# Eight of eleven FFN chunks as seven products in three layers, with the low parts of the two plain weight blocks made by an adding DMA

## The chip, the cores and the metric

The kernel runs on one core of a Trainium2 chip. The metric is device time in microseconds (us) of one execution. TensorE is called PE below, VectorE DVE, ScalarE ACT, GpSimd POOL and SyncE SP; SP issues the loads of the kernel before.

## The reference

A decoder trunk with two layers, one of forgetting attention (FoX) and one of multi-head latent attention (MLA), for 256 tokens of 1024 features in float32. Each layer has two feed-forward networks (FFNs) with 2816 inner columns, so there are four FFNs in all, and they are what the change touches:

```python
def swiglu(x, w_in, w_out):
    h = x @ w_in
    gate, up = h[..., :D_FF], h[..., D_FF:]
    return (jax.nn.silu(gate) * up) @ w_out
...
  x <- LN(alpha*x + 0.5*SwiGLU_1(x))
  x <- LN(alpha*x + Mixer(x))
  x <- LN(alpha*x + 0.5*SwiGLU_2(x))
  x <- LN(alpha*x + sigmoid(x Wg + bg) * (p[i] Wp))
```

## The kernel before

**Split operands.** Every matrix product runs in a reduced float32 format, on operands split into a high part (the value rounded to that format) and a low part (value minus high part). A product is three matmuls: high by high, high by low, low by high. So each block of weights passes two engines before PE can use it: ACT writes the high part (`activation`, Copy, L242 or L250), then DVE subtracts it from the raw block to give the low part (L243 or L254). Both land in one of ten weight slots hl0 to hl9, which PE frees as it goes. Raw groups of 2048 columns (1 MB) arrive by SP's queue into three buffers named raw.

**Chunks.** The 2816 inner columns are cut into 11 chunks of 256. `HT` computes a chunk's gate and up products in turn (gate half, then up half, on PE's `h` and `tr` banks); ACT applies silu to the gate half (L799), DVE multiplies by the up half (L805). The output product of a chunk, its 256 columns by a 256 by 1024 piece of `w_out`, is done in one of two ways:

- plain (`W`): 24 matmuls of 512 columns, at the end of the FFN, on tiles named g and hl;
- summed (`sums`): the 2 by 2 block product as seven products instead of eight, 21 matmuls of 512 columns. For that DVE makes sums and differences of the chunk's blocks (L820, L824, L825, tile P), and ACT and DVE split the result of 896 columns into a *form* (L603 high, L607 low), which stands in one of the home tiles ota, otb, qk and fs. DVE also makes sums of weight blocks by three adds: L274 (1024 columns, into the tile ts), L280 (512, ts) and L282 (512, back into columns 0 to 511 of raw).

The weights of a summed chunk are four units. Unit 0 is columns 0 to 1023 of raw *after* the third add has overwritten their first half; unit 1 is the plain columns 1024 to 2047; units 2 (1024 columns) and 3 (512) are the sums in ts. `WS_ORDER` says in which order PE uses them, and the same order is that in which ACT and DVE prepare them: 1, 0, 2, 3.

**Stages of one FFN.** The chunks come in groups. After the first group PE runs the *first sums*, after the second group (chunks 5, 6, 7) the *second sums*, and then the third group (8, 9, 10), whose chunks are plain. The first FFN of all (*cold*) has chunks 0, 1, 2 plain and sums 3, 4, then 5, 6, 7. The second FFN of layer 0 and that of layer 1 sum 0, 2, 3, 4, then 5, 6, 7, with chunk 1 plain. The first FFN of layer 1 (*kv*) sums 2, 3, 4, then 5, 6, 7, with 0 and 1 plain and three homes. So a sums stage ends with the form of the chunk whose up half PE has finished last, and that chunk's multiplication, form and weights are made while PE runs the products of the chunks ahead of it.

**What sets the order.** `pump` is called after each group of three matmuls (L590 is the matmul in `mm`). It keeps a small model of how far PE, ACT and DVE have got (`pe_t`, `act_t`, `dve_t`) and, when ACT and DVE are at most 1600 ns ahead of PE and a slot is free, emits the next unit's split or the next add. So the order of ACT's and DVE's instructions is fixed when the program is built, and each engine runs its own list in that order. `close` and `T` put the multiplication by the up half and the making of the form into the same lists.

Of the kernel before, what the change touches and what calls it, by code (L numbers as in the profile page):

```python
# [12 lines left out]
AF = mybir.ActivationFunctionType  # L13
ALU = mybir.AluOpType
# [3 lines left out]
NCH = DFF // 256  # L18
# [10 lines left out]
SLACK_NS = 1600.0  # L29
STAG = 3  # L30
# [13 lines left out]
ENDS = ((0, 512), (512, 768), (768, 1024))  # L44
GROUPS = ((2, 3, 4), (5, 6, 7), (8, 9, 10))
HOMES = ("ota", "otb", "qk", "fs")
WS_ORDER = (1, 0, 2, 3)
VRING = ((0, 0), (1, 1), (1, 2), (2, 2))
FOX = (
# [95 lines left out]
class Stream:  # L145


    def __init__(self, nc, raw_pool, pool, loads, seq):
        self.nc, self.raw_pool, self.pool, self.loads = nc, raw_pool, pool, loads
        seen = []  # L150
        self.groups = []
        for key in seq:
            g = group_of(key)
            if g not in seen:
                seen.append(g)
                self.groups.append(g)
# [24 lines left out]
        self.fixed = 80  # L181

    def load(self, n=NRAW):
        while self.loaded < len(self.groups) and self.loaded < self.done + n:
# [78 lines left out]
        self.split_done(key, w)  # L263

    def sums_left(self, key):
        return key[0] == "ws" and self.added.get(group_of(key), 0) < 3

    def add(self, g):

# [38 lines left out]

    def split_done(self, key, w):
        self.hl[key] = w  # L310
        self.ready += 1
        if key in self.last_of:
            self.done = self.last_of[key] + 1
            self.load()
# [42 lines left out]

    def pump(self):

        if self.ready == len(self.order) or not self.slots or self.hold or self.order[self.ready] == self.stop:  # L360
            return
        arrival = self.arrives.get(group_of(self.order[self.ready]), 1e12)
        if arrival <= self.pe_t + 500 and max(self.act_t, self.dve_t) <= self.pe_t + SLACK_NS:
            key = self.order[self.ready]
            if self.sums_left(key):
                self.add(group_of(key))
            else:
                self.split()
# [116 lines left out]
class Trunk:  # L485
# [212 lines left out]
    def ffn(self, li, which, lni, kv=False, ple=False, at=None, cold=False, after=()):  # L698
# [2 lines left out]
        nc, S = self.nc, self.S  # L701
        at = at or {}
        g, gT, forms = {}, {}, {}
        homes = HOMES[:3] if kv else HOMES
        S.reclaim(*homes)
        S.fixed = 150
        early = (0, 1, 2) if cold else (0, 1) if kv else (1,)
        summed = [c for c in range(NCH - STAG) if c not in early]

        def H(c, t, at=None, what=None, sweeps=0):  # L710
# [124 lines left out]
        def sums(chunks, p4):  # L835

            for c in chunks:
# [12 lines left out]
                        c == first, c == last,  # L850
                    )

                for u in WS_ORDER:
                    w = self.use(("ws", li, which, c, u))
                    if u == 0:
                        product(4, 2, w, 0, chunks[0], chunks[-1])
                        if c == chunks[-1]:
                            xs = self.x[0][:, 512:1024]
                            scale = 2 * ALPHA if c != summed[-1] else 1.0
                            nc.vector.scalar_tensor_tensor(xs, xs, scale, y[4], op0=ALU.mult, op1=ALU.add)  # L860
                            S.busy(dve=512)
# [44 lines left out]
        def W(c, ts, what=None):  # L906
            for kt in range(2):
                w = self.use(("wout", li, which, 2 * c + kt))
                for t in ts:
                    for n in range(2):  # L910
                        if kt == 1 and what:
# [5 lines left out]
                            (t, c, kt) == (0, early[0], 0), (c, kt) == (NCH - 1, 1),  # L917
                        )

        both = (0, 1)  # L920
# [17 lines left out]
        n = NCH  # L938
# [7 lines left out]
        for i, group in enumerate((((1,) + GROUPS[0]) if cold else GROUPS[0],) + GROUPS[1:]):  # L946
# [13 lines left out]
            if i < 2:  # L960
                if i == 1 and kv:
                    self.flush()
                sums([c for c in summed if (c < 5) == (i == 0)], ("h", x))
                x = 1 - x
            if i == 1:
                S.lend(*after)
# [840 lines left out]
def tile_trunk(ctx: ExitStack, tc: tile.TileContext, a):  # L1807
# [10 lines left out]
    d = Dummy()  # L1818
    Trunk(d, (d, d), d, r, True).run()
    S = Stream(nc, raw, sb, make_loads(a), r.seq)  # L1820
    Trunk(nc, (sb, ps), a, S, False, dr.tile([16, 256], F32, name="fox_c")).run()


# [79 lines left out]
```

## Time and profile before

| | |
|---|---|
| time, median of 3 runs (lowest to highest) | 1052.56 us (1052.06 to 1052.59) |
| the profiled execution's own time | 1056.31 us |
| its span | 1054.5 us |
| granted TensorE clock, mean | 0.999 |
| PE busy | 1043.3 us (99%), 7097 matmuls |
| DVE busy | 872.7 us (83%), 1280 instructions |
| ACT busy | 584.5 us (55%), 889 instructions |
| POOL busy | 57.5 us (5%), 88 instructions, none of them a DMA |
| bytes by SP's queue | 201.63 MB, 53.9% of the 16 DMA engines' time |

In the timeline rows below the columns are: start in us, duration in us, engine, line of the kernel, operation, output <- inputs, shapes, number of instructions in the row, and in brackets the idle time of the engine ahead of it with what ended it. A row's duration runs to the end of its last instruction; the next instruction of an engine may start a little before the former one has ended, so what an instruction takes on its engine is read from start to start. Times from such a row are times in the profiled execution.

### The profile page before, as it was taken

To read this page: it belongs to the slowest core of one execution; us is meant where nothing else is said; L and a number is where in the kernel's file an instruction comes from. 1 tells how busy PE (TensorE), PEld (TensorE's weight loads), DVE (VectorE), ACT (ScalarE), POOL (GpSimd) and SP (SyncE) were. 2 spreads that over 40 slices of the span, in tenths; PEclk is the share of its full clock that TensorE was granted. 3 is DMA by queue.
4 is the path that set the end of the run, shared out by engine and by line. 5 is a ranking of instruction groups with operands and counts; after the bars stand their busy time and mean duration, and the time that the engine had idled before them with its cause. 6 is when DMAs were issued, how large, how long until landed. Compare 5 with 4: busy or idle time off the path is not lost.

```text
span 1054.5 us, 17598 instructions
## 1 busy us (share of the span) xinstructions
PE 1043.3 (99%) x7097; PEld 955.8 (91%) x7097; DVE 872.7 (83%) x1280; ACT 584.5 (55%) x889; POOL 57.5 (5%) x88
## 2 busy tenths in 40 slices
PE   9999999999999999999999999999999999999996
PEld 8999898999889999998899999988999889899986
DVE  5797976868898989968978898778887989899776
ACT  5555554556745555663564655536776564656621
POOL 0000000122400000000130000000000000000000
PEclk9999999999999999999999999999999999999999
DMA  7765486444637373764574637633444565555622
GB/s 279 284 228 208 160 277 246 155 146 151 221 132 275 139 259 134 256 232 159 179 274 158 240 125 248 235 109 105 151 155 165 188 213 194 199 197 213 208 113 80
DMA packets 37477, 202.75 MB, mean 192 GB/s; under 512 B 3970, under 2 KB 9874, under 8 KB 16532
## 3 DMA queue, kind: packets, MB, share of 16 engines
q1 hardware_dynamic: 37396, 201.63, 53.9%
q8 instruction: 56, 0.92, 0.3%
q14 instruction: 25, 0.20, 0.1%
HBM read 200.55 MB, written 1.06 MB: 191 GB/s over the span
## 4 chain that ended last, share of the span: by engine, by line
PE 71%; DVE 2%; ACT 1%; issue 0%; DVEq 0%; ACTq 0%
PE h L590 37%; PE y L590 23%; PE tr L590 8%; PE tr L594 2%; PE h L594 0%; DVE hl L243 0%; DVE x L682 0%; DVE tr L1688 0%; ACT qk L603 0%; ACT P L1313 0%; DVE h L1295 0%; DVE y L1295 0%; DVE hl L254 0%; ACT xT L1606 0%; DVE PT L607 0%
## 5 line engine op out<-in xcount | busy, mean ns | idle before, releaser
L590 PE MATMUL h<-xT,hl 128*128 128x256 f32 x3384 | 397.0, 279 | 0.2 <-DVE hl L303 0.2
L590 PEld LDWEIGHTS h<-xT,hl 128*128 128x128 f32 x3384 | 393.4, 189 | 1.9 <-ACT xT L603 0.6
L243 DVE TENSOR_TENSOR hl<-raw,hl 128x1024 fp32r<-128x1024 f32 (+3 forms) x289 | 336.3, 1195 | 52.5 <-ACT hl L242 51.1
L242 ACT ACTIVATE hl<-raw 128x1024 fp32r<-128x1024 f32 (+3 forms) x289 | 286.3, 1030 | 75.6 <-PE y L590 31.8
L590 PE MATMUL y<-hl,g 128*128 128x512 f32 x432 | 100.3, 390 | 0.0
L590 PEld LDWEIGHTS y<-hl,g 128*128 128x128 f32 x432 | 80.6, 188 | 16.3
L590 PE MATMUL y<-hl,otb 128*128 128x512 f32 x264 | 70.2, 398 | 0.0
L590 PE MATMUL h<-hl,xT 128*128 128x512 f32 (+2 forms) x300 | 65.2, 370 | 0.0
L590 PEld LDWEIGHTS h<-hl,xT 128*128 128x128 f32 x300 | 52.5, 188 | 9.3
L590 PEld LDWEIGHTS y<-hl,otb 128*128 128x128 f32 x264 | 48.2, 188 | 10.3 <-DVE otb L607 0.3
L254 DVE TENSOR_TENSOR hl<-raw,hl 128x1024 fp32r<-128x1024 f32 (+2 forms) x42 | 50.2, 1199 | 1.5 <-ACT hl L250 1.4
L590 PE MATMUL y<-hl,ota 128*128 128x512 f32 x192 | 49.9, 394 | 0.0
L674 POOL TENSOR_TENSOR rs<-ve,mhalf 128x1 f32<-128x1 f32 x16 | 15.1, 944 | 621.3 <-DVE ve L673 621.3
L590 PE MATMUL y<-hl,xT 128*128 128x512 f32 (+3 forms) x258 | 47.8, 333 | 0.0
L250 ACT ACTIVATE hl<-raw 128x1024 fp32r<-128x1024 f32 (+2 forms) x42 | 43.1, 1029 | 6.8 <-DVE raw L282 5.6
L603 ACT ACTIVATE xT<-tr 128x512 fp32r<-128x512 f32 x28 | 16.2, 597 | 53.2 <-PE tr L594 53.1
L590 PE MATMUL tr<-xT,hl 128*128 128x256 f32 x384 | 45.6, 278 | 0.0
L590 PEld LDWEIGHTS tr<-xT,hl 128*128 128x128 f32 x384 | 44.9, 188 | 0.3
L243 DVE TENSOR_TENSOR hl<-ts,hl 128x1024 fp32r<-128x1024 f32 (+1 forms) x47 | 43.4, 958 | 2.0 <-ACT hl L242 2.0
L799 ACT ACTIVATE P<-h 128x512 f32<-128x512 f32 x33 | 19.7, 598 | 45.1 <-PE h L590 45.0
L590 PEld LDWEIGHTS y<-hl,xT 128*128 128x128 f32 x258 | 39.8, 188 | 4.5 <-ACT xT L603 0.4
L590 PEld LDWEIGHTS y<-hl,ota 128*128 128x128 f32 x192 | 35.0, 188 | 6.6
(284 smaller groups left out, 1442.3 us busy)
## 6 DMA issues: line engine op xcount, KB each, us to landing
raw<-in_ffn_in_dram SPq DMA_DIRECT2D x85, 1024.0 KB, 4.9
raw<-in_ffn_out_dram SPq DMA_DIRECT2D x44, 1024.0 KB, 4.9
raw<-in_pg_dram SPq DMA_DIRECT2D x8, 1024.0 KB, 5.9
raw<-in_mo_dram SPq DMA_DIRECT2D x8, 1024.0 KB, 4.8
raw<-in_kq_dram SPq DMA_DIRECT2D x8, 640.0 KB, 3.9
gb<-in_ln_g_dram SPq DMA_DIRECT2D x8, 512.0 KB, 5.7
gb<-in_ln_b_dram SPq DMA_DIRECT2D x8, 512.0 KB, 6.5
raw<-in_fk_dram SPq DMA_DIRECT2D x4, 1024.0 KB, 5.4
```

What stands on the lines that cost most here:

```text
L242: nc.scalar.activation(hi, src, AF.Copy)
L243: nc.vector.tensor_tensor(lo, src, hi.bitcast(F32), op=ALU.subtract)
L250: nc.scalar.activation(hi, src, AF.Copy)
L254: nc.vector.tensor_tensor(lo, src, hi.bitcast(F32), op=ALU.subtract)
L590: self.nc.tensor.matmul(out, lhsT, rhs, start=start, stop=stop)
L594: self.nc.tensor.transpose(out, in_, self.ident)
L603: self.nc.scalar.activation(hi, src, AF.Copy)
L674: nc.gpsimd.tensor_tensor(rs, ve, self.mhalf, op=ALU.pow)
L799: nc.scalar.activation(gt, ps, AF.Silu)
```

## The change

- A new method `plain` prepares unit 1 in another way, and at another time. ACT writes the high part, as before, and then the *negated* raw block into the place of the low part (`scale=-1.0`; written in the reduced format this is the negated high part). Then POOL issues a DMA that adds the raw block, read from the weights in DRAM a second time (512 KB), onto it. DVE's subtraction for this unit is gone. `plain` is tried first in each call of `pump`, for the first loaded group whose unit 1 has not been issued, and takes a slot at that moment, provided that two are free; so this work stands ahead of the next unit in ACT's list.
- `WS_ORDER` becomes two orders: 2, 3, 0, 1, and for the last chunk of a sums stage 0, 2, 3, 1.
- In the three FFNs other than the cold one no early chunk is plain any more: they sum eight chunks, 0, 2, 3, 4 and then 1, 5, 6, 7. The kv FFN has four homes, as the others. The cold one sums the same five chunks as before.

```diff
-WS_ORDER = (1, 0, 2, 3)
+WS_ORDER = ((2, 3, 0, 1), (0, 2, 3, 1))
...
     def sums_left(self, key):
-        return key[0] == "ws" and self.added.get(group_of(key), 0) < 3
+        return key[0] == "ws" and key[-1] != 1 and self.added.get(group_of(key), 0) < 3
+
+    def plain(self):
+
+        g = next((g for g in self.groups[self.done : self.loaded] if g[0] == "ws" and g not in self.issued), None)
+        if g is None or g + (1,) in self.hl or self.arrives[g] > self.pe_t + 500:
+            return
+        if self.act_t > self.pe_t + SLACK_NS or len(self.slots) < 2:
+            return
+        key = g + (1,)
+        src, _, n = unit_of(key, self.raw[g])
+        slot = self.slots.pop(0)
+        self.slot_of[key] = slot
+        w = self.hl[key] = self.place(key, slot)
+        self.issued.add(g)
+        self.nc.scalar.activation(w[:, 0, :n], src, AF.Copy)
+        self.nc.scalar.activation(w[:, 1, :n], src, AF.Copy, scale=-1.0)
+        self.nc.gpsimd.dma_start(w[:, 1, :n], self.a[g[2]][1][g[1], g[-1]][:, 1024:2048], accum_op=ALU.add)
+        self.busy(act=n)
+        self.busy(act=n)
+        self.skip()
...
     def pump(self):
 
+        if not self.hold:
+            self.plain()
...
-        homes = HOMES[:3] if kv else HOMES
+        homes = HOMES
         S.reclaim(*homes)
         S.fixed = 150
-        early = (0, 1, 2) if cold else (0, 1) if kv else (1,)
+        early = (0, 1, 2) if cold else ()
...
-                for u in WS_ORDER:
+                for u in WS_ORDER[c == chunks[-1]]:
...
-                sums([c for c in summed if (c < 5) == (i == 0)], ("h", x))
+                sums([c for c in summed if (c < 5 and (cold or c != 1)) == (i == 0)], ("h", x))
```

The lines of the changed kernel are shifted: what was L242, L243, L250, L254 is now L243, L244, L251, L255; the adds L274, L280, L282 are L302, L308, L310; L590 is L624; L603 and L607 are L637 and L641; L799, L805, L820, L824, L825 are L834, L840, L855, L859, L860. The new instructions of `plain` are L282 (high part), L283 (negated) and L284 (the DMA). 25 of the 29 summed chunks take this way.

**The end of the second sums in the second FFN of layer 0, ACT.** hl0 to hl9 are the slots (the number behind the name tells apart what stands in a slot at different times). Before, from the preparation of the weights of chunk 6 to the form of chunk 7 (qk, the last of this stage) and the weights of chunk 7, ACT's list is:

```order
L799 ACTIVATE P_4447<-h1_4394 128x512
L242 ACTIVATE hl0_4456<-raw_4240 128x1024
L242 ACTIVATE hl1_4471<-raw_4240 128x1024
L242 ACTIVATE hl4_4486<-ts_4428 128x1024
L242 ACTIVATE hl6_4498<-ts_4428 128x512
L250 ACTIVATE hl5_4516<-raw_4304 128x1024
L603 ACTIVATE qk_4522<-P_4447 128x896
```

In the changed kernel, where this stage has the forms of chunks 1, 5, 6, 7 in ota, otb, qk and fs, it is, from the form of chunk 6 (qk) to that of chunk 7 (fs) and on to unit 0 of chunk 7 (hl9_4607):

```order
L637 ACTIVATE qk_4411<-P_4331 128x896
L282 ACTIVATE hl7_4440<-raw_4259 128x1024
L283 ACTIVATE hl7_4440<-raw_4259 128x1024
L834 ACTIVATE P_4468<-h1_4415 128x512
L282 ACTIVATE hl8_4471<-raw_4320 128x1024
L283 ACTIVATE hl8_4471<-raw_4320 128x1024
L243 ACTIVATE hl5_4487<-ts_4401 128x512
L243 ACTIVATE hl2_4502<-raw_4259 128x1024
L637 ACTIVATE fs_4535<-P_4468 128x896
L282 ACTIVATE hl1_4547<-raw_4393 128x1024
L283 ACTIVATE hl1_4547<-raw_4393 128x1024
L243 ACTIVATE hl4_4565<-ts_4545 128x1024
```

The unit 1 blocks of chunks 5 and 6 (hl7, hl8) now stand ahead of units 3 and 0 of chunk 5 (hl5, hl2), with two activations each.

**The same place, DVE.** In the changed kernel, from units 3 and 0 of chunk 5 to unit 0 of chunk 7:

```order
L244 TENSOR_TENSOR hl5_4487<-ts_4401,hl5_4487 128x512
L244 TENSOR_TENSOR hl2_4502<-raw_4259,hl2_4502 128x1024
L840 TENSOR_TENSOR P_4468<-P_4468,h0_4470 128x512
...
L641 TENSOR_TENSOR fs_4535<-P_4468,fs_4535 128x896
L302 TENSOR_TENSOR ts_4545<-raw_4320 128x1024
...
L244 TENSOR_TENSOR hl4_4565<-ts_4545,hl4_4565 128x1024
L244 TENSOR_TENSOR hl6_4574<-ts_4545,hl6_4574 128x512
L244 TENSOR_TENSOR hl0_4580<-raw_4320,hl0_4580 128x1024
L302 TENSOR_TENSOR ts_4591<-raw_4393 128x1024
L308 TENSOR_TENSOR ts_4591<-ts_4591,raw_4393 128x512
L310 TENSOR_TENSOR raw_4393<-ts_4591,raw_4393 128x512
L244 TENSOR_TENSOR hl9_4607<-raw_4393,hl9_4607 128x1024
```

Before, DVE's list at the end of this stage ran from the third add of chunk 7's group (raw_4304) to its unit 0 (hl3) like this, with unit 1 (hl5), the first that PE used, needing no add:

```order
L282 TENSOR_TENSOR raw_4304<-ts_4509,raw_4304 128x512
L805 TENSOR_TENSOR P_4447<-P_4447,h0_4449 128x512
...
L254 TENSOR_TENSOR hl5_4516<-raw_4304,hl5_4516 128x1024
L607 TENSOR_TENSOR qk_4522<-P_4447,qk_4522 128x896
L243 TENSOR_TENSOR hl3_4554<-raw_4304,hl3_4554 128x1024
L243 TENSOR_TENSOR hl8_4563<-ts_4509,hl8_4563 128x1024
```

The adds stood ahead of the multiplication there; now they stand behind the form, and unit 0 of the last chunk, which PE uses first, comes behind the third of them.

**The end of the first sums in the second FFN of layer 0, ACT.** The last chunk is 4, with its form in fs. Before, and then in the changed kernel, from that form to unit 0 of chunk 4 (hl0_4040 before is its unit 1, hl1_4049 its unit 0; hl3_4060 its unit 0 now):

```order
L603 ACTIVATE fs_3979<-P_3912 128x896
L242 ACTIVATE hl7_4001<-raw_3677 128x1024
L242 ACTIVATE hl2_4010<-ts_3944 128x1024
L242 ACTIVATE hl9_4019<-ts_3944 128x512
L242 ACTIVATE hl0_4040<-raw_3799 128x1024
L242 ACTIVATE hl1_4049<-raw_3799 128x1024
```

```order
L637 ACTIVATE fs_3985<-P_3918 128x896
L282 ACTIVATE hl0_4001<-raw_3682 128x1024
L283 ACTIVATE hl0_4001<-raw_3682 128x1024
L282 ACTIVATE hl5_4008<-raw_3796 128x1024
L283 ACTIVATE hl5_4008<-raw_3796 128x1024
L243 ACTIVATE hl4_4021<-ts_3950 128x512
L243 ACTIVATE hl6_4030<-raw_3682 128x1024
L243 ACTIVATE hl3_4060<-raw_3796 128x1024
```

Four activations for the unit 1 blocks of chunks 3 and 4 (hl0, hl5) stand ahead of units 3 and 0 of chunk 3 (hl4, hl6) now.

**The end of the first sums in the cold FFN, DVE.** Chunk 4 is the last there, with its form in otb. Before, and then in the changed kernel, from the adds of its weight group (raw_557) to the form:

```order
L282 TENSOR_TENSOR raw_557<-ts_739,raw_557 128x512
L243 TENSOR_TENSOR hl4_764<-raw_557,hl4_764 128x1024
L805 TENSOR_TENSOR P_713<-P_713,h1_715 128x512
L820 TENSOR_TENSOR P_713<-P_713 128x256
L824 TENSOR_TENSOR P_713<-P_713 128x128
L825 TENSOR_TENSOR P_713<-P_713 128x128
L254 TENSOR_TENSOR hl5_776<-raw_557,hl5_776 128x1024
L607 TENSOR_TENSOR otb_782<-P_713,otb_782 128x896
```

```order
L310 TENSOR_TENSOR raw_557<-ts_738,raw_557 128x512
L244 TENSOR_TENSOR hl5_763<-raw_557,hl5_763 128x1024
L244 TENSOR_TENSOR hl6_778<-ts_738,hl6_778 128x1024
L840 TENSOR_TENSOR P_723<-P_723,h1_725 128x512
L855 TENSOR_TENSOR P_723<-P_723 128x256
L859 TENSOR_TENSOR P_723<-P_723 128x128
L860 TENSOR_TENSOR P_723<-P_723 128x128
L255 TENSOR_TENSOR hl7_784<-ts_738,hl7_784 128x512
L641 TENSOR_TENSOR otb_790<-P_723,otb_790 128x896
```

One more low part of 1024 columns stands ahead of the multiplication now, and the first one (hl5, unit 0) needs the third add, through ACT, where before it was unit 1 (hl4).

More of the change, by code (lines that the diff above doesn't have):

```diff
@@ L181, in __init__ @@
         self.fixed = 80
+        self.issued = set()
     def load(self, n=NRAW):
@@ L265, in sums_left, with skip @@
     def sums_left(self, key):
-        return key[0] == "ws" and self.added.get(group_of(key), 0) < 3
+        return key[0] == "ws" and key[-1] != 1 and self.added.get(group_of(key), 0) < 3
[17 more added lines that the diff above has]
+        self.skip()
+    def skip(self):
+        while self.ready < len(self.order):
+            key = self.order[self.ready]
+            if key[0] != "ws" or key[-1] != 1 or group_of(key) not in self.issued:
+                return
+            self.finished(key)
     def add(self, g):
@@ L310, in split_done, with finished @@
         self.hl[key] = w
+        self.finished(key)
+        self.skip()
+    def finished(self, key):
         self.ready += 1
@@ L703, in ffn @@
         g, gT, forms = {}, {}, {}
-        homes = HOMES[:3] if kv else HOMES
+        homes = HOMES
         S.reclaim(*homes)
         S.fixed = 150
-        early = (0, 1, 2) if cold else (0, 1) if kv else (1,)
+        early = (0, 1, 2) if cold else ()
+        plain = early + tuple(range(NCH - STAG, NCH))
         summed = [c for c in range(NCH - STAG) if c not in early]
@@ L916, in W @@
                             lambda i: w[:, i, 512 * n : 512 * n + 512],
-                            (t, c, kt) == (0, early[0], 0), (c, kt) == (NCH - 1, 1),
+                            (t, c, kt) == (0, plain[0], 0), (c, kt) == (NCH - 1, 1),
                         )
@@ L1820, in tile_trunk @@
     S = Stream(nc, raw, sb, make_loads(a), r.seq)
+    S.a = a
     Trunk(nc, (sb, ps), a, S, False, dr.tile([16, 256], F32, name="fox_c")).run()
```

## Prediction

> **What bounds the kernel now.** I read the page's busy shares first, then what PE waits for, then the rows around the sums stages.
>
> ```profile
> span 1054.5 us, 17598 instructions
> ...
> PE 1043.3 (99%) x7097; PEld 955.8 (91%) x7097; DVE 872.7 (83%) x1280; ACT 584.5 (55%) x889; POOL 57.5 (5%) x88
> ```
>
> ```profile
> PE y L566 <- POOL mhalf L551: 1.2, 1, 1.2
> ...
> PE h L590 <- DVE hl L303: 0.2, 1, 0.2
> ```
>
> The second fence holds the first and last of five rows of the waits (total, times, longest): PE waits under 3 us in the whole run, and for nothing in the sums stages. So the kernel is bound by PE, and DVE and ACT keep ahead of it. Fewer matmuls save their time; any block that comes later than PE reaches it costs its lateness in full.
>
> **What the change removes: matmuls.** Four more chunks are summed (two in kv, one in each second FFN), each with 21 matmuls for 24.
>
> ```profile
> 375.28 1.52 PE L590 MATMUL y<-hl,fs 128*128 128x512 f32 x6
> ...
> 380.04 0.87 PE L590 MATMUL h<-xT,hl 128*128 128x256 f32 x6
> ...
> 466.28 20.57 PE L590 MATMUL y<-hl,g 128*128 128x512 f32 x90
> 486.68 0.60 PE L594 MATMUL tr<-ident,x 128*128 128x128 f32 x4
> ```
>
> A plain matmul takes (486.68-466.28)/90 = 0.227 us, so a plain chunk 24 x 0.227 = 5.44. A summed chunk with its form in fs, the home that each of these stages adds, takes 380.04-375.28 = 4.76. The gain is 4 x 0.68 = **-2.7 us**. The 25 subtractions that leave DVE (1.13 each from start to start, below) gain nothing by themselves, since PE did not wait for them; what counts is when the blocks at a stage's end are ready.
>
> **What it moves, 1: first sums of the three FFNs.** Rows of before in the second FFN of layer 0, ACT, then DVE:
>
> ```profile
> 355.56 0.60 ACT L799 ACTIVATE P<-h 128x512 f32<-128x512 f32 x1 [0.37 <-PE h L590]
> ...
> 363.00 0.95 ACT L603 ACTIVATE fs<-P 128x896 fp32r<-128x896 f32 x1 [3.72 <-DVE P L825]
> 363.86 1.04 ACT L242 ACTIVATE hl<-raw 128x1024 fp32r<-128x1024 f32 x1
> ```
>
> ```profile
> 357.44 1.23 DVE L274 TENSOR_TENSOR ts<-raw 128x1024 f32<-128x1024 f32 x1
> 358.70 0.69 DVE L280 TENSOR_TENSOR ts<-ts,raw 128x512 f32<-128x512 f32 x1
> 359.43 0.69 DVE L282 TENSOR_TENSOR raw<-ts,raw 128x512 f32<-128x512 f32 x1
> 360.04 1.22 DVE L243 TENSOR_TENSOR hl<-raw,hl 128x1024 fp32r<-128x1024 f32 x1
> 361.17 0.68 DVE L805 TENSOR_TENSOR P<-P,h 128x512 f32<-128x512 f32 x1
> ```
>
> From start to start the adds take 1.26, 0.73 and 0.61, a low part of 1024 columns 1.13, a form's high part 0.86. Silu at 355.56 waits for PE, so it is a fixed point. Behind it ACT now has a block of 1024 columns instead of 512: high part 356.06 to 357.11, low part 357.17 to 358.30, so the adds start at 358.30 instead of 357.44 and the form's high part at 363.86 instead of 363.00. Then ACT runs the form (0.86) and four unit 1 activations (0.95 each, below): 368.52. hl4 takes 0.50, hl6's high part ends at 370.07; DVE idles for it. hl6's low part starts at 370.13, the adds at 371.26, the third ends 2.68 later at 373.94; hl3 needs it: high part 374.00 to 375.05, low part 375.11 to 376.33. PE is at this chunk at 375.28 and wants the low part for the second matmul at 375.51; with 0.06 from engine to engine it gets it at 376.39. **+0.9 us, three times: +2.6.**
>
> **What it moves, 2: second sums of the same FFNs.** ACT, DVE and PE of before:
>
> ```profile
> 397.04 0.60 ACT L799 ACTIVATE P<-h 128x512 f32<-128x512 f32 x1 [0.76 <-PE h L590]
> 397.54 1.05 ACT L242 ACTIVATE hl<-raw 128x1024 fp32r<-128x1024 f32 x1
> ...
> 405.67 0.96 ACT L603 ACTIVATE otb<-P 128x896 fp32r<-128x896 f32 x1 [2.67 <-DVE P L825]
> ...
> 422.17 3.89 ACT L242 ACTIVATE hl<-raw 128x1024 fp32r<-128x1024 f32 x4
> ```
>
> ```profile
> 403.84 0.68 DVE L805 TENSOR_TENSOR P<-P,h 128x512 f32<-128x512 f32 x1
> ...
> 406.66 1.09 DVE L607 TENSOR_TENSOR otb<-P,otb 128x896 fp32r<-128x896 f32 x1 [0.42 <-ACT otb L603]
> 407.67 1.22 DVE L274 TENSOR_TENSOR ts<-raw 128x1024 f32<-128x1024 f32 x1
> ...
> 419.91 1.09 DVE L607 TENSOR_TENSOR qk<-P,qk 128x896 fp32r<-128x896 f32 x1
> ```
>
> ```profile
> 413.16 1.54 PE L590 MATMUL y<-hl,ota 128*128 128x512 f32 x6
> ...
> 422.82 1.56 PE L590 MATMUL y<-hl,qk 128*128 128x512 f32 x6
> ...
> 427.70 0.87 PE L590 MATMUL h<-xT,hl 128*128 128x256 f32 x6
> ```
>
> An activation of 1024 columns steps by (3.89-1.05)/3 = 0.95; a form's high part starts 1.83 after its multiplication (403.84 to 405.67). Before, the last form (qk) was complete at 419.91+1.09 = 421.0, 1.8 ahead of PE. Now: silu 397.04, unit 1 of chunk 1 (hl9) 397.54 to 399.44, hl4's high part ends at 400.49. DVE: hl4 400.55, hl6 401.68, hl0 402.29, adds 403.42, multiplication of chunk 6 at 406.01 (403.84 before, with 0.61 for 512 columns). ACT: form 407.84, hl7 408.70 and 409.65, silu 410.60, hl8 411.09 and 412.04, hl5 412.99, hl2 413.49 to 414.54. DVE has been idle from 409.9 to 413.7; hl2's low part runs to 415.73, and only then comes chunk 7's multiplication, which PE had ready at 413.16. Form: high part 417.56 to 418.51, low part to 419.57; adds to 422.16; hl4, hl6, hl0 to 425.03; the third add of chunk 7's group ends at 427.71; hl9's high part 427.77 to 428.82, low part to 430.10. PE would use it at 427.70 (high) and 427.93 (low), and gets the low part at 430.16: **+2.2 us, three times: +6.7.** The lists of kv and of layer 1's second FFN have the same order here, so I take the same size.
>
> **What it moves, 3: first sums of the cold FFN.**
>
> ```profile
> 55.44 0.96 ACT L603 ACTIVATE ota<-P 128x896 fp32r<-128x896 f32 x1 [4.83 <-DVE P L825]
> ```
>
> ```profile
> 67.03 1.08 DVE L607 TENSOR_TENSOR otb<-P,otb 128x896 fp32r<-128x896 f32 x1
> 68.03 1.82 DVE L243 TENSOR_TENSOR hl<-ts,hl 128x1024 fp32r<-128x1024 f32 x2
> 69.77 1.22 DVE L243 TENSOR_TENSOR hl<-raw,hl 128x1024 fp32r<-128x1024 f32 x1
> ```
>
> ```profile
> 68.64 1.56 PE L590 MATMUL y<-hl,otb 128*128 128x512 f32 x6
> ```
>
> Here otb was ready at 68.11, only 0.5 ahead of PE. Now ACT has hl2 (twice) behind ota, then hl3 and hl4: 56.30, 57.25, 58.20, 58.70, 59.75. DVE: hl4's low part 59.81, adds 60.94, the third ends at 63.62; hl5's high part 63.68 to 64.73, low part 64.79; hl6 65.92; multiplication 67.05; otb high 68.88 to 69.84, low 69.90 to 70.98. PE gets the high part 1.26 late, and the low part, wanted two matmuls later, another 0.7: **+2.0**. The cold second sums lose nothing: the form's subtractions leave DVE there, and the blocks come about 1 us earlier.
>
> **What it adds: the DMAs.** No adding DMA and no DMA from POOL stands in the trace. The nearest rows are loads by SP and POOL's small operation:
>
> ```profile
> raw<-in_kvv_dram SPq DMA_DIRECT2D x4, 512.0 KB, 3.6
> ...
> gb<-in_ln_b_dram SPq DMA_DIRECT2D x8, 512.0 KB, 6.5
> ...
> x<-in_x_dram SPq DMA_DIRECT2D x2, 512.0 KB, 8.3
> ```
>
> ```profile
> L674 POOL TENSOR_TENSOR rs<-ve,mhalf 128x1 f32<-128x1 f32 x16 | 15.1, 944 | 621.3 <-DVE ve L673 621.3
> ```
>
> The tightest of the 25 are the three for chunk 3's unit 1: negated at 366.7, wanted by PE after 15 matmuls of the qk chunk, at 374.1, so 7.3 us. Next come 11 us (hl7: 410.6 to 421.7). Between 3.6 and 6.5 the cost is nothing; at 8.3 plus a POOL step of 0.9 the block is 1.9 late, of which 0.9 would have been waited for anyway: +1.0 each, +3.0. At twice 6.5 plus 0.9 it is 6.5 late, net 5.6 each, and the 11 us blocks come 2.8 late where PE would wait 2.2 anyway, 0.6 each: 3 x 6.2 = +19. Below nothing it can't go, as nothing is taken off PE. I take nothing, since most rows of 512 KB lie at 3.6 to 6.5; both ends stay in the range. POOL's other work (rs, 15.1 us in the layer norms) stands outside the sums stages, so nothing is queued behind a DMA that waits for its negated block. The bytes rise by 25 x 0.5 = 12.5 MB on 201.6 MB.
>
> The rest I cost at nothing: the second activation of the other blocks, and the adds, forms and splits of the four new chunks, lie beside PE's gate and up products, 11 us a chunk (402 to 413 for chunk 7), of which ACT and DVE leave a part idle (ACT is busy 55% of the span). Without that cover each activation would cost 0.95.
>
> The Trainium skill, "DMA: Bandwidth & Descriptors", section "Anatomy of one DMA", gives 2.0 us plus bytes over 436 GB/s for a DMA that POOL issues; as an estimate that is 3.2 us for one of these, and the term would be nothing by it too. The page gives no figure for the adding.
>
> **Sum.** -2.7 + 2.6 + 6.7 + 2.0 = **+8.6 us**. The profiled execution would go from 1056.3 to 1064.9 us; the median of the runs stands 3.8 below it, so 1052.6 + 8.6 = **1061.2 us**, 0.8% slower.
>
> **Rivals.**
> - *Ends of the second sums hold* (for: PE had 1.8 us in hand there; against: the six steps on ACT between form and hl2 have one order). Then -2.7+2.6+2.0 = +1.9, **1054.5**. It decides if hl2's high part comes over 2 us earlier.
> - *No stage end is late*, the other sign: DVE's list is shorter by a subtraction per chunk, and if the blocks stand as far ahead as before (1.8 us at qk), only the matmuls count: **1049.8**. Against it stands the third add, whose way through ACT to DVE (2.4 us) is now ahead of PE's first use.
> - *The adding DMA is slow*: from 7.3 us on each us costs 3; at 9.2 us **1064.2**, at 13.9 about 1080.
> - *POOL's DMA doesn't get out while DVE runs without a gap.* Chunk 4's block, negated at 368.6, would leave when DVE's run from 370.1 to 376.3 ends; with 6.5 it lands at 382.8, wanted at 379.8: +3.0 three times, **1070**. POOL's row can't show it: nothing was issued there. The Trainium skill, "SBUF — State Buffer", section "SBUF: two separate sides", describes such a starving of POOL's descriptors, but for DVE operations that take both ports, such as copies; by that rule the subtractions here, which read two tensors, would not cause it, which speaks for a low chance.
>
> **Chances.** Forecast 0.58; second sums hold 0.13; no end late 0.12; slow DMA 0.12; held DMA 0.05. The range, 1053 to 1069, takes in the first two, and the DMA up to some 11 us; it leaves out the fast case and the slowest DMAs, 2 in 10. About 0.2% (2 us) is what a measurement can tell from no change: faster 0.12, same 0.13, slower 0.75.
>
> **What would show it.** Right: waits of PE on DVE's hl at the last chunk of each sums stage, some 2 us in the second sums and 1 us in the first, and 2 us on otb near 69 us; DVE idle some 4 us on ACT before hl5 near 410. Wrong: PE without waits there, or waits on the DMA's blocks instead.

## The result and the profile after

| | before | changed |
|---|---|---|
| time, median (runs) | 1052.38 us (4) | 1064.91 us (4; 1064.42 to 1065.16) |
| ratio to before, 95% interval | | 1.0119 (1.0101 to 1.0136) |
| span of the profiled execution | 1054.5 us | 1063.4 us |
| matmuls | 7097 | 7085 |

Slower, by 12.5 us, where 8.6 had been forecast (1061.2, range 1053 to 1069). The page of the changed kernel, its first lines and its DMA issues:

```profile
span 1063.4 us, 17727 instructions
...
PE 1042.7 (98%) x7085; PEld 950.9 (89%) x7085; DVE 864.9 (81%) x1287; ACT 617.7 (58%) x926; POOL 79.5 (7%) x113
...
hl<-in_ffn_out_dram POOLq DMA_DIRECT2D x25, 512.0 KB, 5.7
```

DVE is less busy than before (864.9 against 872.7 us), and yet PE now waits for it. The list of PE's waits (total, times, longest) has new first rows:

```profile
PE h L624 <- DVE hl L244: 4.5, 6, 0.8
PE h L624 <- ACT hl L243: 1.6, 3, 0.5
...
PE tr L624 <- DVE hl L244: 1.2, 3, 0.4
PE h L624 <- ACT otb L637: 1.0, 1, 1.0
PE h L624 <- DVE otb L641: 0.6, 2, 0.4
```

All are waits for weight blocks (hl) or for the form of the cold FFN (otb), none for a DMA of POOL. In the cold first sums PE waits for the form of chunk 4, and at the end of layer 0's first sums for unit 0 of chunk 4. PE's rows for the first, then DVE's and PE's for the second:

```profile
68.52 0.72 PE L624 MATMUL h<-hl,otb 128*128 128x512 f32 x2 [1.03 <-ACT otb L637]
69.64 0.50 PE L624 MATMUL h<-hl,otb 128*128 128x512 f32 x1 [0.40 <-DVE otb L641]
```

```profile
374.69 1.23 DVE L244 TENSOR_TENSOR hl<-raw,hl 128x1024 fp32r<-128x1024 f32 x1 [1.18 <-ACT hl L243]
```

```profile
375.98 0.74 PE L624 MATMUL h<-hl,fs 128*128 128x512 f32 x2 [0.71 <-DVE hl L244]
```

The timeline of the second sums in layer 0's second FFN shows how such waits come about; ACT, then DVE, then PE:

```profile
410.47 1.04 ACT L283 ACTIVATE hl<-raw 128x1024 fp32r<-128x1024 f32 x1
411.41 0.58 ACT L834 ACTIVATE P<-h 128x512 f32<-128x512 f32 x1
411.89 1.05 ACT L282 ACTIVATE hl<-raw 128x1024 fp32r<-128x1024 f32 x1
412.84 1.05 ACT L283 ACTIVATE hl<-raw 128x1024 fp32r<-128x1024 f32 x1
413.79 0.62 ACT L243 ACTIVATE hl<-ts 128x512 fp32r<-128x512 f32 x1
414.31 1.05 ACT L243 ACTIVATE hl<-raw 128x1024 fp32r<-128x1024 f32 x1
```

```profile
409.68 1.08 DVE L641 TENSOR_TENSOR qk<-P,qk 128x896 fp32r<-128x896 f32 x1
414.44 0.69 DVE L244 TENSOR_TENSOR hl<-ts,hl 128x512 fp32r<-128x512 f32 x1 [3.68 <-ACT hl L243]
415.39 1.23 DVE L244 TENSOR_TENSOR hl<-raw,hl 128x1024 fp32r<-128x1024 f32 x1 [0.26 <-ACT hl L243]
416.53 0.68 DVE L840 TENSOR_TENSOR P<-P,h 128x512 f32<-128x512 f32 x1
...
427.79 0.69 DVE L310 TENSOR_TENSOR raw<-ts,raw 128x512 f32<-128x512 f32 x1
429.65 1.23 DVE L244 TENSOR_TENSOR hl<-raw,hl 128x1024 fp32r<-128x1024 f32 x1 [1.17 <-ACT hl L243]
```

```profile
413.77 0.86 PE L624 MATMUL tr<-hl,ota 128*128 128x512 f32 x3
...
424.21 0.73 PE L624 MATMUL tr<-hl,qk 128*128 128x512 f32 x2 [0.38 <-DVE hl L244]
424.78 0.87 PE L624 MATMUL y<-hl,qk 128*128 128x512 f32 x3
...
429.67 0.49 PE L624 MATMUL h<-hl,fs 128*128 128x512 f32 x1 [0.53 <-ACT hl L243]
430.93 0.72 PE L624 MATMUL h<-hl,fs 128*128 128x512 f32 x2 [0.77 <-DVE hl L244]
```

DVE stands idle for 3.68 us in the middle of the stage, while ACT works through the unit 1 blocks. The multiplication of chunk 7 comes at 416.53, 2.8 us after PE had its half ready (413.77). From there DVE has two gaps: 1.02 us for the high part of the form, and 1.17 us for ACT behind the third add. PE waits at three places.

Where the time went, by stage: from the start of the first to that of the last matmul of each stage, in the two profiled executions, in us. "Plain" are the plain chunks' products (`W`).

| stage | before | after | change |
|---|---|---|---|
| cold, first sums | 9.41 | 11.39 | +1.98 |
| cold, second sums | 14.40 | 14.30 | -0.10 |
| layer 0, second FFN: first sums | 19.07 | 20.10 | +1.03 |
| second sums | 14.31 | 21.62 | +7.31 |
| plain | 27.19 | 21.75 | -5.44 |
| kv: first sums | 14.31 | 20.05 | +5.74 |
| second sums | 14.31 | 21.64 | +7.33 |
| plain | 27.89 | 17.01 | -10.88 |
| layer 1, second FFN: first sums | 19.06 | 20.41 | +1.35 |
| second sums | 14.31 | 21.60 | +7.29 |
| plain | 27.20 | 21.76 | -5.44 |
| sum | | | **+10.2** |

The stages between these differ by under 0.3 us, but for the start up to the first sums (63.9 before, 62.6 after), one stretch of layer 0's mixer (0.8 shorter after) and the end of the program, whose lines in the kernel the change leaves alone. From the landing of the last output to the end of the program it is 0.97 us before and 1.79 after: SP closes the program with waits for semaphores, and there are more of them with the adding DMAs (nine such instructions in place of five). In the five traces without these DMAs (before, before_again, order_alone, no_dma, one_order_no_dma) this stretch takes 0.94 to 0.97 us, in the seven with them 1.72 to 1.79. So the DMAs cost 0.8 us there, 14 of them as much as 25.

### The profile page after: what moved, and what is told of

It is laid out like the page before. It is cut to its first block, busy times and chain, and to the rows that moved or that the text cites. A ratio compares the mean times of both kernels' runs of the same rounds, so it can differ in the third digit from the quotient of the medians.

```text
span 1063.4 us, 17727 instructions
## 1 busy us (share of the span) xinstructions
PE 1042.7 (98%) x7085; PEld 950.9 (89%) x7085; DVE 864.9 (81%) x1287; ACT 617.7 (58%) x926; POOL 79.5 (7%) x113
## 4 chain that ended last, share of the span: by engine, by line
PE 58%; DVE 11%; ACT 5%; issue 3%; DVEq 0%; ACTq 0%
PE h L624 30%; PE y L624 19%; PE tr L624 7%; DVE hl L244 5%; ACT hl L243 2%; PE tr L628 2%; DVE ts L302 1%; ACT hl L282 1%; DVE ts L308 1%; ACT hl L283 1%; DVE raw L310 1%; DVE P L840 1%; DVE P L855 0%; DVE P L860 0%; DVE P L859 0%
## 5 line engine op out<-in xcount | busy, mean ns | idle before, releaser
L624 PE MATMUL h<-xT,hl 128*128 128x256 f32 x3384 | 395.2, 278 | 0.7 <-ACT hl L329 0.6
L624 PEld LDWEIGHTS h<-xT,hl 128*128 128x128 f32 x3384 | 391.5, 188 | 2.5 <-ACT hl L329 1.2
L244 DVE TENSOR_TENSOR hl<-raw,hl 128x1024 fp32r<-128x1024 f32 (+4 forms) x271 | 314.3, 1191 | 54.2 <-ACT hl L243 52.9
L243 ACT ACTIVATE hl<-raw 128x1024 fp32r<-128x1024 f32 (+4 forms) x271 | 268.5, 1027 | 88.2 <-PE y L624 31.2
L624 PE MATMUL y<-hl,g 128*128 128x512 f32 x336 | 78.6, 391 | 0.0
L624 PEld LDWEIGHTS y<-hl,g 128*128 128x128 f32 x336 | 62.5, 188 | 12.6
L624 PE MATMUL y<-hl,otb 128*128 128x512 f32 x264 | 69.0, 398 | 0.0
L624 PE MATMUL h<-hl,xT 128*128 128x512 f32 (+2 forms) x312 | 68.2, 371 | 0.0
L244 DVE TENSOR_TENSOR hl<-ts,hl 128x512 fp32r<-128x512 f32 (+1 forms) x51 | 46.0, 927 | 24.9 <-ACT hl L243 24.9
L624 PEld LDWEIGHTS h<-hl,xT 128*128 128x128 f32 x312 | 54.8, 188 | 9.9
L624 PEld LDWEIGHTS y<-hl,otb 128*128 128x128 f32 x264 | 48.2, 188 | 10.1 <-DVE otb L641 0.3
L624 PE MATMUL y<-hl,xT 128*128 128x512 f32 (+3 forms) x282 | 52.7, 334 | 0.0
L284 POOL DMA_DIRECT2D hl<-in_ffn_out_dram x25 | 21.8, 873 | 403.7 <-ACT hl L283 185.3
L243 ACT ACTIVATE hl<-ts 128x512 fp32r<-128x512 f32 (+1 forms) x51 | 40.0, 813 | 18.8 <-DVE ts L302 18.8
L624 PE MATMUL y<-hl,ota 128*128 128x512 f32 x192 | 48.6, 393 | 0.0
L624 PEld LDWEIGHTS y<-hl,xT 128*128 128x128 f32 x282 | 44.1, 188 | 4.6 <-ACT xT L637 0.4
L637 ACT ACTIVATE xT<-tr 128x512 fp32r<-128x512 f32 x28 | 16.1, 596 | 52.3 <-PE tr L628 52.3
L624 PE MATMUL tr<-xT,hl 128*128 128x256 f32 x384 | 45.6, 279 | 0.0
L624 PEld LDWEIGHTS tr<-xT,hl 128*128 128x128 f32 x384 | 44.9, 188 | 0.3
L255 DVE TENSOR_TENSOR hl<-raw,hl 128x1024 fp32r<-128x1024 f32 (+2 forms) x36 | 42.5, 1184 | 1.0 <-ACT hl L251 0.9
L624 PEld LDWEIGHTS y<-hl,ota 128*128 128x128 f32 x192 | 35.5, 188 | 7.2
```

Of the source, the lines that this page charges most:

```text
L243: nc.scalar.activation(hi, src, AF.Copy)
L244: nc.vector.tensor_tensor(lo, src, hi.bitcast(F32), op=ALU.subtract)
L255: nc.vector.tensor_tensor(lo, src, hi.bitcast(F32), op=ALU.subtract)
L284: self.nc.gpsimd.dma_start(w[:, 1, :n], self.a[g[2]][1][g[1], g[-1]][:, 1024:2048], accum_op=ALU.add)
L624: self.nc.tensor.matmul(out, lhsT, rhs, start=start, stop=stop)
L637: self.nc.scalar.activation(hi, src, AF.Copy)
```

## The experiments

**The kernel before, once more.** The two spans differ by 8.9 us, the medians by 12.5, and the stages by 10.2.

> The kernel before, unchanged, profiled once more. The changed kernel's rows account for +8.9 us between the two spans (1054.5 to 1063.4), the medians for +12.5. Theory: the first profiled execution of before was a slow one (1056.3 against a median of 1052.4), with over 1 us of it ahead of the first sums stage; then this one has a span near 1051 and the first sums stage begins near 62.5 us instead of 63.9. Rival: every profiled execution of before carries some 4 us that the changed kernel's does not; then its span is 1054 to 1055 again.

Measured: 1051.69 us, span 1049.9. The first matmuls of the first sums, in this trace:

```profile
60.66 1.54 PE L590 MATMUL y<-hl,ota 128*128 128x512 f32 x6
```

They had started at 63.87 in the first profile: 3.2 us of the 4.6 that the two spans of one program differ lie ahead of them. So the profiled execution on which the prediction was made was a long one, and the stage table, not the spans, tells what the change costs.

**One order for all chunks.**

```diff
-WS_ORDER = ((2, 3, 0, 1), (0, 2, 3, 1))
+WS_ORDER = ((2, 3, 0, 1), (2, 3, 0, 1))
```

> One edit on the changed kernel: the last chunk of a sums stage takes its units in the order 2, 3, 0, 1 like the others, so its first unit needs the first add alone and unit 0 comes nine matmuls (2.1 us) later. Theory (the waits at the ends of the stages come from unit 0 standing first behind the third add): the wait at the last chunk of the second sums falls from 1.7 to some 0.6, that of the first sums from 0.9 or 1.2 to nothing, cold first sums from 1.75 to 0.7: 6 to 7 us faster than the changed kernel, about 1058.5. Rival (adding DMAs or their traffic make the loss): no change, 1065.

Measured: 1061.23 us (1059.97 to 1062.71), 3.7 us faster than the changed kernel: a little over half of what was expected. PE's waits:

```profile
PE h L628 <- DVE x L895: 4.2, 7, 1.6
PE tr L624 <- DVE hl L244: 2.4, 6, 0.9
```

The waits for blocks fell as expected (7.3 us of hl rows to 2.4, and otb's from 1.6 to 0.6). A new one has come: L628 is the first transpose of the next group of chunks, which needs the bank h (where PE's results stand until they are read) that product 4, made from unit 0, has filled, and L895 is DVE's reading of that bank. That is what unit 0 at the front of the last chunk is good for: it empties the bank early.

**Unit 1 first.**

```diff
-WS_ORDER = ((2, 3, 0, 1), (0, 2, 3, 1))
+WS_ORDER = ((2, 3, 0, 1), (1, 2, 3, 0))
```

> One edit on the changed kernel: the last chunk's order is 1, 2, 3, 0, so the block that the DMA completed long before comes first and unit 0, behind the third add, last. Theory A (only the lateness of the blocks counts): the waits inside the sums stages go except some 0.6 at the chunk ahead, 7 us faster, about 1058. Theory B (product 4, made from unit 0, must be read out of its PSUM bank by DVE before the next group of chunks may use that bank; unit 0 at the very end moves the wait there): the waits inside the stages go as in A, but new ones of 1.4 to 2.3 us stand at the first transposes behind each sums stage, and the time stays within 1 us of 1065.

Measured: 1070.43 us (1069.84 to 1072.66), 5.5 us slower than the changed kernel.

```profile
PE h L628 <- DVE x L895: 11.5, 7, 2.1
PE tr L624 <- DVE hl L244: 1.3, 4, 0.5
```

Theory B is right about the place: the waits for blocks are nearly gone, and more than they were stands at the bank, 11.5 us against the 8.9 of the rows for hl and otb in the changed kernel. The time came out beyond both theories for that reason, and because two of these waits were followed by a stretch at half the clock (below). The windows behind the one at 657.84 (us, busy time of PE, PEld, DVE, ACT and POOL with instructions, granted clock, DMA share, GB/s):

```profile
658.00:660.00 2.00, 2.00 (x16) 2.00 (x16) 0.98 (x2) 1.49 (x3) 0.00 (x0) 0.81 1.01 320
660.00:662.00 2.00, 2.00 (x12) 2.00 (x11) 1.91 (x2) 1.49 (x3) 0.00 (x0) 0.50 0.87 369
662.00:664.00 2.00, 2.00 (x16) 2.00 (x16) 2.00 (x4) 0.57 (x1) 0.00 (x0) 0.83 0.54 143
```

**The adding DMAs left out.**

```diff
-        self.nc.gpsimd.dma_start(w[:, 1, :n], self.a[g[2]][1][g[1], g[-1]][:, 1024:2048], accum_op=ALU.add)
```

> The changed kernel with the 25 adding DMAs left out: the low parts of these blocks stay the negated high parts, so the output is not the reference's; all other instructions and their order remain. Theory (the DMAs are hidden: they land 5.7 us after issue, the tightest place has 7.3): within 0.5 us of the changed kernel, 1065. Rival (13 MB more traffic, or POOL's queue, delays the loads or PE): 2 us or more faster.

Measured: 1064.85 us (1062.47 to 1066.50), the changed kernel's time, as far as runs that spread over 4 us can tell. The six sums stages of the three other FFNs take the same within 0.1 us in the two traces. So in the changed kernel's sums stages the DMAs are covered; the 0.8 us at the end of the program are too little for these runs to show.

**The same in one_order.** This asks what one_order's waits at the bank come from.

> one_order with the 25 adding DMAs left out, so the low parts of these blocks stay the negated high parts and the output is not the reference's. In one_order PE waits 4.2 us for product 4's bank, where DVE's read-out stands behind low parts whose weights ACT got late from a load that ran beside two adding DMAs (median landing 6.3 us in that stretch, 5.0 in the kernel before). Theory (the adding DMAs slow the loads there): the landings fall to 5 us, the waits on the read-out to about 1 us, and the time by 2 to 4 us, to 1057 to 1059. Rival (the order alone makes the read-out late): within 1 us of one_order, 1061.

Measured: 1057.47 us (1056.47 to 1058.45), 3.8 us faster than one_order; the waits on the read-out fell from 4.2 to 1.2, and the end of the program is 0.8 us shorter, which together make the difference. The loads at three places (windows around the first sums' ends) landed in medians of 6.1 to 6.5 us with the adding DMAs and 5.3 to 5.8 without. At one of them, in kv, ACT in one_order and then without the DMAs:

```profile
594.89 2.00 ACT L243 ACTIVATE hl<-raw 128x1024 fp32r<-128x1024 f32 x2 [2.57 <-DMA raw<-in_ffn_in_dram]
```

```profile
592.04 2.01 ACT L243 ACTIVATE hl<-raw 128x1024 fp32r<-128x1024 f32 x2 [0.43 <-DMA raw<-in_ffn_in_dram]
```

The load for which ACT waits here took 8.1 us from issue to landing beside two adding DMAs, and 6.0 without them. DVE's low part of this block stands ahead of its read-out of the bank, and so a load that is 2 us later holds up PE. The changed kernel has such late loads too: the first one behind the two DMAs took 7.1 to 7.8 us at the three places, against 4.8 to 5.0 in the last version (combined2, below), which has no adding DMA there. So the second read of the weights is free only where other waits leave the loads time.

**The order alone.** On the kernel before, with no unit 1 work on ACT and no DMA:

```diff
-WS_ORDER = (1, 0, 2, 3)
+WS_ORDER = ((2, 3, 0, 1), (0, 2, 3, 1))
...
-                for u in WS_ORDER:
+                for u in WS_ORDER[c == chunks[-1]]:
```

> The kernel before with one part of the change alone: the two orders of the units (2, 3, 0, 1, and 0, 2, 3, 1 for the last chunk). No second activation, no adding DMA, the chunk sets of before. Theory (in the second FFNs and kv the waits come from ACT's doubled activations, put ahead of the next units; the order hurts by itself only in the cold FFN, where the form of chunk 4 is 0.5 us ahead of PE): some 1.3 us lost at the cold first sums and up to 1 at the cold second sums, nothing elsewhere: 1 to 3 us slower than before, 1053 to 1055. Rival (unit 0 first behind the third add is the whole cause): waits of 2 us at the end of each second sums and 1 us at each first sums, some 10 us slower, 1062.

Measured: 1054.79 us, ratio to before 1.0021 (1.0011 to 1.0031): some 2 us, as the theory had it, with PE waiting 1.1 us for otb and 0.8 us for hl. The rival (unit 0 first as the whole cause) falls.

**The change without the added chunks.** In it the chunk sets and homes are those of before:

```diff
-        homes = HOMES
+        homes = HOMES[:3] if kv else HOMES
...
-        early = (0, 1, 2) if cold else ()
+        early = (0, 1, 2) if cold else (0, 1) if kv else (1,)
...
-                sums([c for c in summed if (c < 5 and (cold or c != 1)) == (i == 0)], ("h", x))
+                sums([c for c in summed if (c < 5) == (i == 0)], ("h", x))
```

> The change without the four added chunks: the second activation, the adding DMA and the two orders, with the chunk sets of before. The prediction's steps give 2 us in the cold first sums, 0.9 in the first sums of the second FFNs, and 1.7 to 2 at the last chunk of each second sums, in that FFN and in kv, against no gain in matmuls: 8 to 10 us slower than before, 1060 to 1062. Rival (the eighth chunk is what overloads ACT and DVE): within 3 us of before.

Measured: 1063.86 us, ratio 1.0105 (1.0087 to 1.0123). That is 11 us over before, with no chunk added, against 2 us for the order alone: the unit 1 work carries 9 us in this setting. One wait, of 1.9 us in kv, is here for an adding DMA. The expectation missed in one place: kv's second sums lost nothing (14.31 us, as before). The four chunks are not what overloads DVE: with them the changed kernel has about the same time (the two intervals overlap), so what they save, 2.7 us, goes in stalls at the ends that they lengthen: the second sums of the three FFNs lose 1.7, nothing and 1.7 us without the added chunks, and 2.5 to 2.6 each with them.

**Unit 1 work behind the regular units.** `pump` is split in two:

```diff
     def pump(self):
 
-        if not self.hold:
+        if not self.regular() and not self.hold:
             self.plain()
+
+    def regular(self):
+
         if self.ready == len(self.order) or not self.slots or self.hold or self.order[self.ready] == self.stop:
-            return
+            return False
...
                 self.split()
+            return True
+        return False
```

> One edit on the changed kernel: pump first emits the next unit's split or add, and only where it emits none tries the two activations and the DMA of unit 1. Theory (ACT's doubled activations ahead of units 3 and 0 make DVE idle and everything behind it late): the waits of the second sums in the three FFNs fall from 2.3 us to under 0.5; those of the first sums, 0.9 to 1.2, and of the cold FFN remain, as unit 0 still stands first behind the third add: 6 to 8 us faster than the changed kernel, 1057 to 1059. Rival (the order is the cause): no change, 1065.

Measured: 1056.93 us (1056.03 to 1058.15), ratio to before 1.0039 (1.0025 to 1.0053): 8 us of the 12.5 gone by the place of the unit 1 work, two activations for each block, in ACT's list. The waits of the second sums in the three FFNs are away; of the waits for blocks and forms that remain, the main row is:

```profile
PE h L629 <- DVE hl L244: 3.0, 4, 0.8
```

They stand at the last chunk of the first sums and in the cold FFN, as expected: unit 0 there still waits for the third add.

**Both cures, and the cold FFN as before.** On plain_second:

```diff
-WS_ORDER = ((2, 3, 0, 1), (0, 2, 3, 1))
+WS_ORDER = ((2, 3, 0, 1), (2, 0, 3, 1))
...
-        g = next((g for g in self.groups[self.done : self.loaded] if g[0] == "ws" and g not in self.issued), None)
+        g = next((g for g in self.groups[self.done : self.loaded] if g[0] == "ws" and g[1:3] != (0, "ffn1") and g not in self.issued), None)
...
-        if self.act_t > self.pe_t + SLACK_NS or len(self.slots) < 2:
+        if self.act_t > self.pe_t + 800 or len(self.slots) < 2:
...
-                for u in WS_ORDER[c == chunks[-1]]:
+                for u in (1, 0, 2, 3) if cold else WS_ORDER[c == chunks[-1]]:
```

`sums_left` keeps its old condition for the cold FFN.

> The changed kernel with what the runs so far point to: the unit 1 work behind the regular units in pump, and only while ACT's model is at most 800 ns ahead; order 2, 0, 3, 1 for the last chunk (its first unit needs one add only, and product 4 still leaves its bank with 15 matmuls to go); the cold FFN left as in the kernel before. If the waits at the ends of the stages and at product 4's bank are all that the change loses, only the 12 matmuls fewer remain: -2.5 us, 1049.8. If the second read of the weights by the adding DMAs delays the loads of the next stage, as one_order hints (loads at 7.2 us instead of 4.9 behind the first sums), 1 to 3 us come back and it ends at 1050 to 1053.

Measured: 1062.16 us (1059.87 to 1066.25), ratio 1.0090 (1.0071 to 1.0109): a miss by 10 us. No wait for a block of DVE over 0.2 us and none at the bank is left, but there is one of another kind:

```profile
PE y L629 <- DMA hl<-in_ffn_out_dram: 4.9, 3, 2.3
```

The unit 1 work of chunk 4 had been pushed back: its adding DMA was issued 9.7 to 10.1 us behind the start of the first sums, where the changed kernel has it at 8.2 to 8.6, and now behind the first load of the next stage. Around the three ends of the first sums both kinds landed in 7.2 to 8.1 us (medians), and chunk 4's DMA, the one that PE waits for, in 9.1 to 10.7, against 6.3 to 6.5 in the changed kernel. The clock made it worse. PE and the windows around the wait in kv:

```profile
593.25 1.54 PE L629 MATMUL y<-hl,fs 128*128 128x512 f32 x5 [2.10 <-DMA hl<-in_ffn_out_dram]
```

```profile
592.00:594.00 2.00, 0.75 (x3) 0.66 (x4) 1.94 (x3) 0.00 (x0) 0.00 (x0) 1.00 1.04 397
594.00:596.00 2.00, 2.00 (x10) 1.81 (x10) 0.41 (x1) 1.50 (x2) 0.00 (x0) 0.60 0.93 336
596.00:598.00 2.00, 2.00 (x12) 2.00 (x11) 2.00 (x3) 1.11 (x2) 0.00 (x0) 0.55 0.91 360
```

Over the 4 us from 594 to 598 the mean granted clock is 0.57, worth another 1.7 us. Two whole stretches of gate and up products, in kv the one behind this wait and in layer 1's second FFN the last one, also ran at the slower pace that the last section describes, some 1.2 us each.

**The last version.** Chunks 3 and 4 keep DVE's subtraction for unit 1, and the limit is pump's own again:

```diff
-        g = next((g for g in self.groups[self.done : self.loaded] if g[0] == "ws" and g[1:3] != (0, "ffn1") and g not in self.issued), None)
+        g = next((g for g in self.groups[self.done : self.loaded] if g[0] == "ws" and g[1:3] != (0, "ffn1") and g[3] not in (3, 4) and g not in self.issued), None)
...
-        if self.act_t > self.pe_t + 800 or len(self.slots) < 2:
+        if self.act_t > self.pe_t + SLACK_NS or len(self.slots) < 2:
```

> combined with two differences: chunks 3 and 4, the last two of the first sums, keep DVE's subtraction for unit 1 (19 DMAs become 13), and the limit for the unit 1 work is pump's own 1600 ns. In combined PE waited 4.9 us for three adding DMAs at the end of the first sums, and the granted clock fell to 0.5 to 0.6 for some 3.5 us behind the two longest of these waits. Theory (that is all that combined lost): no wait over 0.3 us in any sums stage, no stretch at half clock behind one, and the gain of the 12 matmuls remains: -2.5 us, 1050.3 against 1052.9. Rival (the added traffic or ACT's load costs something elsewhere): 1052 to 1055.

Measured: 1051.46 us (1050.37 to 1053.50, 11 runs) against 1052.85 (15 runs), ratio 0.9988 (0.9979 to 0.9996), with 14 adding DMAs. No wait in a sums stage is left among PE's waits, whose longest rows are those that the kernel before has too:

```profile
PE y L605 <- POOL mhalf L590: 1.2, 1, 1.2
PE h L629 <- DVE PT L646: 0.7, 2, 0.5
PE h L629 <- ACT p L642: 0.5, 1, 0.5
```

In its trace each sums stage of four chunks takes 19.07 us, as the undisturbed one of before, and the plain products 21.75, 17.01 and 21.75. So the 2.7 us of the matmuls are there, stage by stage; the medians show 1.4, and the interval (0.4 to 2.2 us) does not reach 2.7. Of the difference, 0.8 us are the longer end of the program that every kernel with adding DMAs has. The remaining 0.5 lies within the interval; in this trace a cold stretch of equal instructions took 1.2 us longer than in before_again (see the last section), but one trace is not the median.

## Why the prediction was right, point by point

- **What bounds the kernel.** PE, with DVE and ACT ahead of it: right, and so was the rule drawn from it, that a late block costs its lateness. A lighter DVE (872.7 to 864.9 us busy) gained nothing.
- **The matmuls, -2.7 us.** The plain stages fell by 5.44, 10.88 and 5.44, and the four chunks come back at 4.76 each: -21.76 + 19.04 = -2.72.
- **First sums, +0.9 three times.** Measured 1.03, 0.98 (5.74 less a chunk of 4.76) and 1.35: 3.4 for 2.6. In layer 0 the lateness itself is as worked out: the last low part ends at 375.92, and PE takes it at 375.98, 0.9 behind its turn (374.86 and one matmul of 0.23). In layer 1 the form, at which the steps begin, came 0.3 later against PE than in layer 0.
- **Second sums, +2.2 three times.** Measured 2.55, 2.57 and 2.53 (each less 4.76): 7.7 for 6.7. The steps fell where they were put: DVE idle for 3.68 us before hl5 (3.8 worked out), chunk 7's multiplication 2.8 us behind PE (2.6), the last low part complete at 430.88, which is 0.2 later relative to PE. What lacked besides is that PE does not pick up its pace at once behind a wait: the two matmuls at 430.93 take 0.57 to the next start, at 431.50, where the steady pace is 0.46 for two.
- **Cold first sums, +2.0.** Measured 1.98, with the two waits for otb's high and low part that were worked out. The cold second sums lost nothing (-0.10), as forecast.
- **The adding DMAs, nothing.** Right for the sums stages of the changed kernel: the landing took 5.7 us in the median, within the 3.6 to 6.5 of the rows, and 5.3 to 5.7 for the three of chunk 3, where 7.3 were to be had; no_dma has the same time. What was put at nothing without a row is the 0.8 us at the end of the program. And the cover is the stalls themselves: with those of the order gone, the DMAs cost 3.8 us, these 0.8 among them (one_order_no_dma), and pushed later they stop PE (combined). The prediction named the price of a late DMA, and not the price for the loads beside it.
- **The sum.** The stages give +10.2 for +8.6, and the end of the program 0.8. The other 1.5 of the 12.5 us stay open, as the timed runs have no trace; the profiled execution of before was longer than its runs by 3.8 us, and the four runs of the changed kernel lie within 0.8 us. That the profiled execution of the changed kernel took 1065.2 us, where the sum had 1064.9, is luck: its starting point, 1056.3, was one of the long executions.
- **The rivals.** "No stage end is late" was wrong: seven of the eight ends were, all but the cold second sums. "Second sums hold" fell with the 3.68 us of idle DVE. The slow DMA fell with the median landing of 5.7 us. The held DMA fell too: the DMA issued at 421.61 landed 5.5 us later, and in all that time DVE had no gap over 0.04 us; by the Trainium skill, "SBUF — State Buffer", section "SBUF: two separate sides", these subtractions should not starve POOL's descriptors, and the trace agrees.
- **What was not foreseen** is a reason for the new orders: unit 0 at the front of the last chunk frees product 4's bank. Taking it away for the sake of the blocks moved the wait to the bank (unit1_first).

## What to carry to other kernels

An engine that is 55% busy on the mean is not free at the place where its list is in the path: doubling its work on some blocks, ahead of others, left the next engine idle for 3.7 us, and 8 of the 12.5 us came back by putting that work behind the regular units. Before work is shifted from one engine to another, follow the list of both from the last fixed point (here a silu that waits for PE) to the first use on the bound engine. And an order that looks wrong for one resource may be right for another: before changing it, ask which buffer it empties.

## What the runs showed of the hardware that was not expected

**The clock behind a wait of PE.** PE's waits of 2.06, 2.10, 2.13 and 2.29 us (two in unit1_first, two in combined) were each followed, within some 2 us, by a stretch of 3.4 us at a granted clock of about 0.5, in which it lost some 1.7 us. Waits of 1.97, 1.90, 1.85 and 1.64 us (unit1_first, plain_alone) were not. No run varies the length of a wait alone, so these are observations and not a measured threshold. The Trainium skill, "TensorE: Matmul & The Clock Gate", section "Part 1: The HAM clock gate (the "warmup" mystery)", puts the return to half clock behind an idle window of some 3.4 us; here 2.1 us were enough, and the slow stretch is what has that length.

**An adding DMA** of 512 KB from DRAM onto a block in SBUF, issued by POOL, landed in 5.7 us (median of 25; 5.3 to 10.6), as a plain load of 512 KB by SP did before (gb, 5.7). Beside four or five loads of 1 MB in combined the medians are 7.3 to 8.1 us for the adding DMAs and 7.2 to 7.7 for the loads of in_ffn_in, where those of before_again took 5.0 to 5.6 at the same places.

**Two lengths of one stage.** The products between the cold FFN's first and second sums, with the same matmuls, took 34.59 us in three traces (before, the changed kernel, combined2) and 33.35 in the nine others, at a granted clock of 1.00 each time. The time is not lost at one place: a matmul of 256 columns steps by 0.118 us (median) through the whole stretch in the long traces, and by 0.113 in the others. The two stretches in combined named above, 36.15 us in kv and 35.29 in layer 1 for 33.35 and 34.05 in before, ran at 0.118 too; the one in kv also holds the stretch at half clock. Why PE keeps the one pace or the other is open. In the two traces of the kernel before, this stretch and the start of the program make 4.5 of the 4.6 us by which the spans differ.
